# A transformer layer on one core: where the second norm's modulation row is computed, and how the first pieces are loaded

## The chip, the cores and the metric

The kernel runs on one core of one Trainium2 chip. The metric is the device time of one execution in microseconds; the median of three runs stands in the section on the profile. The names of the engines are those of the profile: PE (matmul), PEld (its weight load), DVE (VectorE), ACT (ScalarE), POOL (GpSimd) and SP, which here only issues transfers.

## The reference

One layer over 256 latent tokens and 256 context tokens of width 2048. A conditioning vector gives six modulation chunks of 2048 values by one matrix product each; the branches read a normed and modulated input.

```python
def adaln(cond, w_ada, b_ada):
    return jnp.split(jax.nn.silu(cond) @ w_ada + b_ada, 6, axis=-1)

m_lat, m_ctx = adaln(c, w_ada, b_ada), adaln(c_ctx, w_ada, b_ada)
hc = modulate(rms_norm(ctx, norm1_g), m_ctx[0], m_ctx[1])     # h * (1 + scale) + shift
h  = modulate(rms_norm(x, norm1_g), m_lat[0], m_lat[1])
# pc = hc @ w_in[:, :3072], p = h @ w_in -> keys and values of both, queries and gates of h
o_a = gqa(...)         # 16 heads of 128, 4 key heads, rotary
o_b = diff_attn(...)   # 8 heads; each head's output goes through rms_norm(o, subln_g)
merged = sigmoid(g_a) * (o_a @ w_br_a) + sigmoid(g_b) * (o_b @ w_br_b)
x = x + m_lat[2] * (merged @ w_out)
h = modulate(rms_norm(x, norm2_g), m_lat[3], m_lat[4])        # shift is chunk 3
x = x + m_lat[5] * ((silu(h @ w_ff_gate) * (h @ w_ff_up)) @ w_ff_down)
```

## The kernel before

Every large product goes over weight tiles of 128 x 1024 fp32 (two k-tiles of 128 rows by 512 columns, 512 KB). A tile is loaded by SP into the ring `wraw` (7 buffers), ACT casts it to a high part `whi` (L235), DVE subtracts to get the low part `wlo` (L237), and PE makes three matmuls of 512 columns for each product (L241, L242, L243): high by high, high by low, low by high. The stages follow each other on PE: first the keys and values of latent and context tokens, for which x is modulated on the way (to about 145 us); queries, gates, and the attention of branch B, then of branch A (to about 806 us); the merge, `o_a @ w_br_a` times its gate; the output projection (four groups of 512 columns, 8 weight tiles each, from about 894 to 982 us); then the feed-forward. A scheduler places the instructions of each engine in the order of the code with priorities. Each engine, and SP's queue of transfers, works in order.

**The first modulation chunks (`ada_cond`, L280 to L340).** Chunks 0 and 1 are computed in six steps of `STEPS = ((0, 1), (1, 1), (2, 2), (4, 4), (8, 4), (12, 4))`, (first k-tile, how many), each step just before its columns are needed. A step takes two parts (shift and scale), and for each part the conditioning vectors `cst` times pieces of the matrix, 16 matmuls `ada` (L314). A piece is 512 KB in a host-arranged tensor `ada_t`. The steps of 4 k-tiles have 8 pieces to a part, 2 matmuls to each. In all three of these steps, pieces 0 and 1 share a tile of the pool `big`, pieces 2 and 3 go in halves of 256 KB into four small tiles `wada1` of the scratch tags `nr` (2 buffers) and `p` (4 buffers), and pieces 4 to 7 into `wraw`. All 16 matmuls are issued together after the last piece. Tag `p` also holds the tables `cs` and `used` that POOL reads when it makes the rope tables (`rp_kb` and others).

**The later chunks (`ada_pieces`, `ada_row`).** Chunks 2, 4 and 3, and during the feed-forward chunk 5, are made in 32 pieces of 512 KB each. A piece is loaded into `wraw` (L453), and DVE multiplies it by one value of the vector and adds it to a tile `ada` (`SCALAR_TENSOR_TENSOR`, L459) behind the latest wlo. After the last piece PE sums over the partitions (`adac`), DVE adds the bias, and POOL writes the row to DRAM and broadcasts it (`ada_everywhere`). The generator `later` holds chunks 2, 4, 3; `take(later, 1)` advances it by one step, of which a piece has one. `side_work` calls it on each turn of the attention that has nothing else to do: every second turn before branch A's attention is done in its data (`a_done`), and two of three after; the merge calls it too, but nothing is left by then. `b_all`, the broadcast shift of the second norm, is read by `norm2` at the end of the output projection.

**The output of branch B (L826 to L846).** For each of 16 units PE makes `o`, ACT copies it to `on` and sums its squares (`sso`), DVE scales and shifts the sum to `rstdo` (L123), POOL raises it to the power -1/2 (L124), ACT multiplies `on` by it (L842), and PE transposes `on`.

Of the kernel before, what the change touches and what calls it, by code (L numbers as in the profile page):

```python
# [41 lines left out]
TURN2 = 5  # L42
# [4 lines left out]
def hybrid_block(ctx: ExitStack, tc: tile.TileContext, t: dict, out: bass.AP):  # L47
    nc = tc.nc

    big = ctx.enter_context(tc.tile_pool(name="big", bufs=BIG))  # L50
    wp = ctx.enter_context(tc.tile_pool(name="wp", bufs=3))
# [6 lines left out]
    def big_tile(name, dt=F32):  # L58
        return big.tile([P, 2048], dt, tag="big", name=name)
# [7 lines left out]
    def s_ps(name="s"):  # L67
        return psum.tile([P, CG], F32, tag="s", bufs=2, name=name)

    def scratch(name, n=CG, dt=F32, tag="scr", bufs=3):  # L70
        return scr.tile([P, n], dt, tag=tag, bufs=bufs, name=name)
# [137 lines left out]
        nc.vector.tensor_scalar(out=neglam, in0=neglam, scalar1=-LAM_INIT, scalar2=None, op0=ALU.add)  # L209


    last_hi, last_lo = [], []

    def load_raw(r0, c0, n=2):
        raw = wp.tile([P, WK, CG], F32, tag="wraw", bufs=WRAW, name="wraw")
# [5 lines left out]

    def load_w(src, r0, c0, nk=WK, in_big=False):
        raw = wp.tile([P, WK, CG], F32, tag="wraw", bufs=WRAW, name="wraw")
        nc.sync.dma_start(out=raw[:, 0:nk], in_=src[r0:r0 + nk * P, c0:c0 + CG].rearrange("(k p) c -> p k c", p=P))
        return split_w(raw, nk, in_big)

    def split_w(raw, nk, in_big=False, late=None):
# [52 lines left out]
    def ada_cond(k0, nk):  # L280
        ncol = nk * P
        kk = 2 * CG // ncol
        n0 = k0 * P * 2 * D // (P * 2 * CG)
        mod = []
        for part in range(2):
            aps = s_ps("ada")
            held = []
            for q in range(0, NKT, kk):
                piece = t["ada_t"][n0].rearrange("p (k c) -> p k c", c=ncol)
                n0 += 1  # L290
                n = q // kk
                if nk < 4 or n > 3:
                    wt = wp.tile([P, 2 * CG], F32, tag="wraw", bufs=WRAW, name="wada").rearrange("p (k c) -> p k c", c=ncol)
                    nc.sync.dma_start(out=wt, in_=piece)
                elif n < 2:
                    if n == 0:
                        two = big_tile("wada2").rearrange("p (n k c) -> p n k c", n=2, c=ncol)
                    wt = two[:, n]
                    nc.sync.dma_start(out=wt, in_=piece)
                else:  # L300
                    wt = [scratch("wada1", tag=tag, bufs=b) for tag, b in (("nr", 2), ("p", 4))]
                    for j in range(2):
                        nc.sync.dma_start(out=wt[j], in_=piece[:, j, :])
                held += [(q + j, wt[j] if nk == 4 and 1 < n < 4 else wt[:, j, :]) for j in range(kk)]
                last = q + kk == NKT
                if k0 and not last:
                    if nk == 4 and n == 3:
                        yield None
                    continue
                for k, rhs in held[::-1] if k0 else held:  # L310
                    g = k % 4
                    early, late_k = k < 4, k >= NKT - 4
                    with tc.issue_after(last_pe[0].ins) if k0 == 1 and k == held[-1][0] else nullcontext():
                        last_pe[0] = nc.tensor.matmul(aps[32 * g:32 * g + 32, 0:ncol], lhsT=cst[:, k, :], rhs=rhs,  # L314
                                                      start=late_k if k0 else early, stop=early if k0 else late_k)
                held = []
                if last:
                    asb = scratch("asb")
                    last_asb.append(nc.scalar.copy(out=asb[:, 0:ncol], in_=aps[:, 0:ncol]))
                yield None  # L320
                if last:
                    atp = tp_ps("atp")
                    for j in range(nk):
                        nc.tensor.transpose(out=atp[:, j * P:(j + 1) * P], in_=asb[:, j * P:(j + 1) * P], identity=ident)
                    m = small(f"mod{part}", 8)
                    mv = m[:, 0:2 * nk].rearrange("p (j w) -> p j w", w=2)
                    nc.vector.tensor_reduce(
                        out=mv, in_=atp[:, 0:ncol].rearrange("p (j g m) -> p j m g", g=4, m=32)[:, :, 0:2, :],
                        axis=AX.X, op=ALU.add)
# [213 lines left out]
    a_done = []  # L543
# [258 lines left out]
    def back(br, u, pr):  # L802

        grp, hh = unit(br, u)
        if br == "a":
            if hh % 2 == 0:
                pair[:] = [big_tile("pT", F32R).rearrange("p (k c) -> p k c", k=4) for _ in range(2)]
            pT = list(pair)
        else:
            pT = scratch("pT", tag="pTb", bufs=2).rearrange("p (k c) -> p k c", k=4)  # L810
        for i, p in enumerate(pr):
            tp = tp_ps("ptp")
            for kt in range(4):
                nc.tensor.transpose(out=tp[:, kt * P:(kt + 1) * P], in_=p[:, kt * P:(kt + 1) * P], identity=ident)  # L814
            src = tp.rearrange("p (k q) -> p k q", k=4)
            if br == "a":
                c0 = hh % 2 * SEQ + i * P
                split(*[x[:, :, c0:c0 + P] for x in pT], src)
            else:
                nc.scalar.copy(out=pT, in_=src)  # L820
        yield None
        if br == "a" and hh % 2 == 0:
            return
        op = tp_ps("o")
        if br == "a":
            for kt in range(4):  # L826
                vh, vl = [v[:, kt, grp * AD:(grp + 1) * AD] for v in v_a]
                mm3(op, vh, vl, pT[0][:, kt, :], pT[1][:, kt, :], kt == 0, kt == 3)
            last_o.append(nc.scalar.copy(out=o_raw(grp * 4 + hh - 1, 2), in_=op))
            return  # L830
        vb = acc["vb"][grp].rearrange("p (t c) -> p t c", c=CG)
        tk = u % 2
        on = scratch("on", BV, tag="on", bufs=2)
        for kt in range(4):
            nc.tensor.matmul(op[:, 0:BV], lhsT=pT[:, kt, :], rhs=vb[:, kt, hh * BV:(hh + 1) * BV], start=(kt == 0), stop=(kt == 3))  # L835
        nc.scalar.copy(out=on, in_=op[:, 0:BV])
        junk = scratch("junk_o", tag="sq", bufs=2)
        ss = small("sso", 1)
        nc.scalar.activation(out=junk[:, 0:BV], in_=on, func=AF.Square, accum_out=ss)
        r = rstd_of(ss, 1, BV, "rstdo")  # L840
        yield None
        nc.scalar.mul(out=on, in_=on, mul=r)  # L842
        yield None
        tp = tp_ps("otp")
        nc.tensor.transpose(out=tp[:, 0:P], in_=on, identity=ident)
        nc.scalar.mul(out=o_raw(AH + grp * 4 + hh)[:, tk * P:(tk + 1) * P], in_=tp[:, 0:P], mul=gsub)  # L846
# [15 lines left out]
    turns = [0]  # L862
# [3 lines left out]
    def side_work():  # L866

        if next(chores[-1], chores[-1]) is chores[-1] and not quiet:
            turns[0] += 1
            take(later, 1 if turns[0] % (3 if a_done else 2) else 0)  # L870

    q_order = [("b", g) for g in range(2)] + [("a", g) for g in range(4)]
    others = [(gate_d[w], xT, 0, w_in, (GA0, GB0)[w], cg) for w in range(2) for cg in range(4)]
# [35 lines left out]
    for n, (br, u) in enumerate(units):  # L909
        q = (br, unit(br, u)[0])  # L910
# [31 lines left out]
    w_bra, w_out = t["w_br_a"][0], t["w_out"][0]  # L942
    mT = Parts("mT", NKT)
    for cg in range(4):
# [35 lines left out]
        for k, _ in enumerate(project(w_bra, oT, AH, cg * CG, gated)):  # L980
# [5 lines left out]
                    assert not work  # L986
                    o_parts(3)
            take(gates, 1 if cg else (0, 0, 0, 0, 2, 2, 3, 0)[k])
    drain(later)
    b_all = ada_everywhere("b_all", 2)  # L990


    xn = [big_tile(f"xn{i}") for i in range(2)]
# [78 lines left out]
            take(norm2_of[1], 2)  # L1072

    for cg in range(4):
        drain(project(w_out, mT, NKT, cg * CG, out_evac(cg), **(dict(tail=TURN2, hook=tail_hook, in_big=(6, 7)) if cg == 3 else {})))


    NFT = DFF // P
# [103 lines left out]
```

## Time and profile before

| what | value |
|---|---|
| three runs | 1702.79, 1704.09 (median), 1705.93 us |
| profiled execution | 1703.83 us, of which the span is 1701.7 us |
| granted clock of PE over the span | 0.997 |
| PE / PEld busy | 99% / 80% |
| DVE / ACT / POOL busy | 67% / 46% / 12% |
| mean rate of the transfers | 243 GB/s |
| DVE, wlo and ada | 498 of 1.22 us, 120 of 1.28 us on average |

The profile is of one execution. Its page names each group of instructions as `line engine operation out<-in`, with buffer numbers left out. In a timeline the number in brackets is the time for which the engine stood idle before the instruction, with what ended it. A clock below 1.00 means that PE's matmuls were spaced further apart.

### The profile page before, as it was taken

The numbers are of one execution on the slowest core, as the hardware profiler recorded it, in microseconds if no ns is written. First come the engines' busy times: TensorE is split into PE (matmuls) and PEld (weight loads), VectorE is DVE, ScalarE is ACT, GpSimd is POOL, SyncE is SP. The second block draws the span as 40 slices with busy tenths as digits, with TensorE's granted clock in tenths as the row PEclk, the third lists the DMA queues.
The fourth block names the chain that finished last, engine by engine and source line by source line (L and its number), as shares of the span: only waits on it lengthen the run. The fifth ranks groups of instructions, "written<-read, shape, count | busy, mean of one in ns | idle before, by whom it ended". The sixth has DMA issues, their size and how long they took to land.

```text
span 1701.7 us, 21519 instructions
## 1 busy us (share of the span) xinstructions
PE 1676.8 (99%) x7889; PEld 1355.1 (80%) x7889; DVE 1138.4 (67%) x1438; ACT 779.0 (46%) x1071; POOL 209.3 (12%) x296
## 2 busy tenths in 40 slices
PE   7999999999999999999999999999999999999998
PEld 5677778887887778888888888888888888888887
DVE  5665779798687878996666755566666666554454
ACT  5221222246666656577544534444444444333332
POOL 0200002011231210011111101111111111100000
PEclk9999999999999999999999999999999999999999
DMA  9787875778766768776777857788888888766662
GB/s 352 288 316 275 304 253 157 234 252 256 246 180 216 222 225 272 246 238 212 256 265 237 294 175 221 235 263 267 263 272 263 269 274 253 238 218 195 216 207 88
DMA packets 181860, 413.08 MB, mean 243 GB/s; under 512 B 15065, under 2 KB 16298, under 8 KB 181498
## 3 DMA queue, kind: packets, MB, share of 16 engines
q1 hardware_dynamic: 169482, 374.17, 67.3%
q0 software_dynamic: 12272, 37.53, 7.4%
q8 instruction: 62, 1.02, 0.3%
q14 instruction: 44, 0.36, 0.1%
HBM read 395.35 MB, written 16.29 MB: 242 GB/s over the span
## 4 chain that ended last, share of the span: by engine, by line
PE 75%; issue 10%; DVE 6%; DMA 4%; POOL 3%; ACT 2%; SPq 0%; POOLq 0%; DVEq 0%; ACTq 0%
PE mm L241 22%; PE mm L242 22%; PE mm L243 22%; DVE wlo L237 2%; PE ada L314 1%; POOL fturn L1091 1%; ACT whi L235 1%; PE ptp L814 1%; DMA turn_d<-fpart 1%; DMA fturn<-turn_d 1%; DMA wraw<-in_w_in_dram 1%; DVE ada L459 1%; PE mm L401 1%; PE o L835 1%; DVE mx L736 1%
## 5 line engine op out<-in xcount | busy, mean ns | idle before, releaser
L237 DVE TENSOR_TENSOR wlo<-wraw,whi 128x1024 fp32r<-128x1024 f32 x498 | 606.8, 1220 | 443.9 <-ACT whi L235 442.9
L235 ACT CAST whi<-wraw 128x1024 fp32r<-128x1024 f32 x498 | 522.4, 1050 | 714.0 <-PE mm L243 607.2
L242 PE MATMUL mm<-wlo,hT 128*128 128x512 f32 x684 | 266.3, 389 | 0.1
L243 PE MATMUL mm<-whi,hT 128*128 128x512 f32 x684 | 266.1, 389 | 0.0
L241 PE MATMUL mm<-whi,hT 128*128 128x512 f32 x684 | 266.1, 389 | 0.0
L241 PE MATMUL mm<-whi,xT 128*128 128x512 f32 x630 | 252.7, 402 | 1.3 <-ACT xT L359 1.2
L242 PE MATMUL mm<-wlo,xT 128*128 128x512 f32 x630 | 247.0, 392 | 4.3 <-DVE wlo L237 4.3
L243 PE MATMUL mm<-whi,xT 128*128 128x512 f32 x630 | 246.9, 392 | 0.0
L459 DVE SCALAR_TENSOR_TENSOR ada<-wada,vt,ada 128x1024 f32<-128x1024 f32 x120 | 152.0, 1277 | 0.0
L242 PEld LDWEIGHTS mm<-wlo,hT 128*128 128x128 f32 x684 | 128.4, 188 | 27.7 <-DVE wlo L237 0.9
L241 PEld LDWEIGHTS mm<-whi,hT 128*128 128x128 f32 x684 | 128.4, 188 | 26.7
L243 PEld LDWEIGHTS mm<-whi,hT 128*128 128x128 f32 x684 | 128.4, 188 | 26.5
L241 PEld LDWEIGHTS mm<-whi,xT 128*128 128x128 f32 x630 | 118.6, 188 | 32.7 <-issue 7.0
L242 PEld LDWEIGHTS mm<-wlo,xT 128*128 128x128 f32 x630 | 118.8, 189 | 28.2 <-DVE wlo L237 5.7
L243 PEld LDWEIGHTS mm<-whi,xT 128*128 128x128 f32 x630 | 118.5, 188 | 26.0 <-DVE xT L360 0.3
L241 PE MATMUL mm<-whi,fT 128*128 128x512 f32 x354 | 137.5, 388 | 0.5 <-DVE y L1127 0.5
L242 PE MATMUL mm<-wlo,fT 128*128 128x512 f32 x354 | 137.3, 388 | 0.0
L243 PE MATMUL mm<-whi,fT 128*128 128x512 f32 x354 | 137.3, 388 | 0.0
L241 PEld LDWEIGHTS mm<-whi,fT 128*128 128x128 f32 x354 | 66.4, 188 | 15.0 <-issue 0.8
L243 PEld LDWEIGHTS mm<-whi,fT 128*128 128x128 f32 x354 | 66.5, 188 | 13.8
L242 PEld LDWEIGHTS mm<-wlo,fT 128*128 128x128 f32 x354 | 66.4, 188 | 13.7
L241 PE MATMUL mm<-whi,oT 128*128 128x512 f32 x192 | 75.9, 396 | 0.0
(236 smaller groups left out, 2150.4 us busy)
## 6 DMA issues: line engine op xcount, KB each, us to landing
wraw<-in_w_in_dram SPq DMA_DIRECT2D x159, 512.0 KB, 4.7
wada<-in_w_ada_dram SPq DMA_DIRECT2D x128, 512.0 KB, 4.6
wraw<-in_w_ff_gate_dram SPq DMA_DIRECT2D x88, 512.0 KB, 4.6
wraw<-in_w_ff_up_dram SPq DMA_DIRECT2D x88, 512.0 KB, 5.4
wraw<-in_w_ff_down_dram SPq DMA_DIRECT2D x88, 512.0 KB, 4.8
wada<-in_ada_t_dram SPq DMA_DIRECT2D x52, 512.0 KB, 7.8
wraw<-in_w_br_a_dram SPq DMA_DIRECT2D x32, 512.0 KB, 5.3
wraw<-in_w_out_dram SPq DMA_DIRECT2D x32, 512.0 KB, 5.2
```

Of the source, the lines that this page charges most:

```text
L235: last_hi.append(nc.scalar.copy(out=hi[:, 0:nk], in_=raw[:, 0:nk]))
L237: last_lo.append(nc.vector.tensor_tensor(out=lo[:, 0:nk], in0=raw[:, 0:nk], in1=hi[:, 0:nk].bitcast(F32), op=ALU.subtract))
L241: nc.tensor.matmul(ps, lhsT=ah, rhs=wh, start=first, stop=False, skip_group_check=skip)
L242: nc.tensor.matmul(ps, lhsT=ah, rhs=wl, start=False, stop=False, skip_group_check=skip)
L243: return nc.tensor.matmul(ps, lhsT=al, rhs=wh, start=False, stop=last, skip_group_check=skip)
L314: last_pe[0] = nc.tensor.matmul(aps[32 * g:32 * g + 32, 0:ncol], lhsT=cst[:, k, :], rhs=rhs, start=late_k if k0 else early, stop=early if ...
L401: last_pe[0] = nc.tensor.matmul(ps[cg], lhsT=x, rhs=ws0[cg][y], start=(n == 0), stop=(n == 2))
L459: nc.vector.scalar_tensor_tensor(out=dst, in0=wt, scalar=sc[:, 0, kt:kt + 1], in1=dst, op0=ALU.mult, op1=ALU.add)
L736: nc.vector.tensor_reduce(out=mx, in_=sp, axis=AX.X, op=ALU.max, negate=True)
L814: nc.tensor.transpose(out=tp[:, kt * P:(kt + 1) * P], in_=p[:, kt * P:(kt + 1) * P], identity=ident)
L835: nc.tensor.matmul(op[:, 0:BV], lhsT=pT[:, kt, :], rhs=vb[:, kt, hh * BV:(hh + 1) * BV], start=(kt == 0), stop=(kt == 3))
L1091: nc.gpsimd.dma_start(out=whole[32 * b:32 * b + 32].rearrange("p (k a j) -> p k a j", k=4, a=4), in_=blocks[b])
```

## The change

Four edits, with this effect on the order of the instructions:
- The step of the k-tiles 4 to 7 takes all 8 pieces of a part through `wraw`, and its matmuls come in two batches of 8, after pieces 3 and 7 (`first_ks` and `last_ks` set where the accumulation starts and stops). In the two last steps the halves of pieces 2 and 3 go into `nr` twice, `sq` and `pTb` instead of `nr`, `nr`, `p`, `p`, and their loads are put behind the last weight tile's load.
- The multiplication by `rstdo` is done on DVE, as `TENSOR_SCALAR`, instead of on ACT.
- In the attention, every third turn takes a step of `later`.
- In the output projection, each of the steps of the first two groups takes a step of `later`; what is left of it and the broadcast `b_all` come ahead of the third group.

```diff
-    last_hi, last_lo = [], []
+    last_hi, last_lo, last_load = [], [], []
...
-        nc.sync.dma_start(out=raw[:, 0:nk], in_=src[...])
+        last_load.append(nc.sync.dma_start(out=raw[:, 0:nk], in_=src[...]))
...
-                if nk < 4 or n > 3:
-                    wt = wp.tile([P, 2 * CG], F32, tag="wraw", ...)
-                    nc.sync.dma_start(out=wt, in_=piece)
...
-                    wt = [scratch("wada1", tag=tag, bufs=b) for tag, b in (("nr", 2), ("p", 4))]
+                with tc.issue_after(last_load[-1].ins) if k0 >= 8 else nullcontext():
+                    if k0 < 8 or n > 3:
+                        wt = wp.tile([P, 2 * CG], F32, tag="wraw", ...)
+                        nc.sync.dma_start(out=wt, in_=piece)
...
+                        wt = [scratch("wada1", tag=tag, bufs=2) for tag in (("nr", "nr") if n == 2 else ("sq", "pTb"))]
...
-                if k0 and not last:
-                    if nk == 4 and n == 3:
+                if k0 and not last and (k0 != 4 or n != 3):
+                    if k0 >= 8 and n == 3:
                         yield None
                     continue
+                first_ks, last_ks = (range(0, 4), range(12, 16)) if k0 == 0 else (range(4, 8), range(8, 12)) if k0 == 4 else (range(12, 16), range(0, 4))
...
-                                                      start=late_k if k0 else early, stop=early if k0 else late_k)
+                                                      start=k in first_ks, stop=k in last_ks)
...
-        nc.scalar.mul(out=on, in_=on, mul=r)
+        nc.vector.tensor_scalar(out=on, in0=on, scalar1=r, scalar2=None, op0=ALU.mult)
...
-            take(later, 1 if turns[0] % (3 if a_done else 2) else 0)
+            take(later, 1 if turns[0] % 3 == 0 else 0)
...
-    drain(later)
-    b_all = ada_everywhere("b_all", 2)
...
     for cg in range(4):
-        drain(project(w_out, mT, NKT, cg * CG, out_evac(cg), ...))
+        if cg == 2:
+            drain(later)
+            b_all = ada_everywhere("b_all", 2)
+        for _ in project(w_out, mT, NKT, cg * CG, out_evac(cg), ...):
+            take(later, 1)
```

SP's queue in the first 60 us, at the step of the k-tiles 4 to 7. `wraw` is a weight tile, `wada` a piece in the ring, and `wada_737` to `wada_860` are halves of pieces in small tiles. Before:

```order
L224 DMA wraw<-in_w_in_dram 128x2x512
L303 DMA wada_737<-in_ada_t_dram 128x512
L303 DMA wada_738<-in_ada_t_dram 128x512
L303 DMA wada_741<-in_ada_t_dram 128x512
L303 DMA wada_742<-in_ada_t_dram 128x512
L224 DMA wraw<-in_w_in_dram 128x2x512
L294 DMA wada<-in_ada_t_dram 128x1024
L303 DMA wada_860<-in_ada_t_dram 128x512
L294 DMA wada<-in_ada_t_dram 128x1024 x3
```

And now (lines of the changed file are shifted by one):

```order
L224 DMA wraw<-in_w_in_dram 128x2x512
L295 DMA wada<-in_ada_t_dram 128x1024 x4
L224 DMA wraw<-in_w_in_dram 128x2x512
L295 DMA wada<-in_ada_t_dram 128x1024
L170 DMA tok_t_686<-in_x_t_dram 128x1024
L170 DMA tok_t_686<-in_ctx_t_dram 128x1024
L295 DMA wada<-in_ada_t_dram 128x1024 x3
L224 DMA wraw<-in_w_in_dram 128x2x512
L295 DMA wada<-in_ada_t_dram 128x1024 x4
```

The halves are gone from this step, and four whole pieces stand ahead of its weight tile.

DVE in branch B's attention, at the run of work ahead of the matmul at 574.93 us. `mm` is a finished projection whose norm and rotary position (`ss`, `nr`, `sq`) are made here. Before:

```order
L237 TENSOR_TENSOR wlo<-wraw,whi 128x1024
L123 TENSOR_SCALAR rstdo<-sso 128x1
L459 SCALAR_TENSOR_TENSOR ada_2770<-wada_5070,vt,ada_2770 128x1024
L492 TENSOR_REDUCE ss<-sq 128x4
L501 TENSOR_TENSOR nr<-mm,rp_qa 128x512
```

And now:

```order
L460 SCALAR_TENSOR_TENSOR ada_2800<-wada_4966,vt,ada_2800 128x1024
L237 TENSOR_TENSOR wlo<-wraw,whi 128x1024
L123 TENSOR_SCALAR rstdo<-sso 128x1
L843 TENSOR_SCALAR on<-on,rstdo 128x128
L493 TENSOR_REDUCE ss<-sq 128x4
L502 TENSOR_TENSOR nr<-mm,rp_qa 128x512
```

The piece has moved to before the wlo, and the multiplication stands between `rstdo` and the rest of the run.

DVE at the seam of the merge and the output projection, where `m` and `gin` are the merge's products, `mT` the transposed result. Before:

```order
L237 TENSOR_TENSOR wlo<-wraw,whi 128x1024 x4
L966 TENSOR_TENSOR gin<-mm,gin 128x512 x2
L967 TENSOR_TENSOR m_7823<-m_7823,gin 128x512
L967 TENSOR_TENSOR m_7893<-m_7893,gin 128x512
L237 TENSOR_TENSOR wlo<-wraw,whi 128x1024 x2
L247 TENSOR_TENSOR mT_8012<-mtp,mT_8012 128x4x128
```

And now:

```order
L460 SCALAR_TENSOR_TENSOR ada_6631<-wada_7924,vt,ada_6631 128x1024
L237 TENSOR_TENSOR wlo<-wraw,whi 128x1024
L967 TENSOR_TENSOR gin<-mm,gin 128x512 x2
L968 TENSOR_TENSOR m_7759<-m_7759,gin 128x512
L968 TENSOR_TENSOR m_7829<-m_7829,gin 128x512
L460 SCALAR_TENSOR_TENSOR ada_6631<-wada_7962,vt,ada_6631 128x1024
L237 TENSOR_TENSOR wlo<-wraw,whi 128x1024
L247 TENSOR_TENSOR mT_7958<-mtp,mT_7958 128x4x128
L460 SCALAR_TENSOR_TENSOR ada_6631<-wada_7990,vt,ada_6631 128x1024
```

An ada now stands by each wlo, where before there was none. 28 pieces have moved to these two stages, 16 to the merge and 12 to the projection.

More of the change, by code (lines that the diff above doesn't have):

```diff
@@ L223, in load_w @@
         raw = wp.tile([P, WK, CG], F32, tag="wraw", bufs=WRAW, name="wraw")
-        nc.sync.dma_start(out=raw[:, 0:nk], in_=src[r0:r0 + nk * P, c0:c0 + CG].rearrange("(k p) c -> p k c", p=P))
+        last_load.append(nc.sync.dma_start(out=raw[:, 0:nk], in_=src[r0:r0 + nk * P, c0:c0 + CG].rearrange("(k p) c -> p k c", p=P)))
         return split_w(raw, nk, in_big)
@@ L291, in ada_cond @@
                 n = q // kk
-                if nk < 4 or n > 3:
[L293 to L300, printed above, removed]
-                    wt = [scratch("wada1", tag=tag, bufs=b) for tag, b in (("nr", 2), ("p", 4))]
-                    for j in range(2):
-                        nc.sync.dma_start(out=wt[j], in_=piece[:, j, :])
@@ L304, in ada_cond @@
-                held += [(q + j, wt[j] if nk == 4 and 1 < n < 4 else wt[:, j, :]) for j in range(kk)]
+                with tc.issue_after(last_load[-1].ins) if k0 >= 8 else nullcontext():
+                    if k0 < 8 or n > 3:
+                        wt = wp.tile([P, 2 * CG], F32, tag="wraw", bufs=WRAW, name="wada").rearrange("p (k c) -> p k c", c=ncol)
+                        nc.sync.dma_start(out=wt, in_=piece)
+                    elif n < 2:
+                        if n == 0:
+                            two = big_tile("wada2").rearrange("p (n k c) -> p n k c", n=2, c=ncol)
+                        wt = two[:, n]
+                        nc.sync.dma_start(out=wt, in_=piece)
+                    else:
+                        wt = [scratch("wada1", tag=tag, bufs=2) for tag in (("nr", "nr") if n == 2 else ("sq", "pTb"))]
+                        for j in range(2):
+                            nc.sync.dma_start(out=wt[j], in_=piece[:, j, :])
@@ L305, in ada_cond @@
+                held += [(q + j, wt[j] if k0 >= 8 and 1 < n < 4 else wt[:, j, :]) for j in range(kk)]
                 last = q + kk == NKT
-                if k0 and not last:
-                    if nk == 4 and n == 3:
+                if k0 and not last and (k0 != 4 or n != 3):
+                    if k0 >= 8 and n == 3:
                         yield None
                     continue
+                first_ks, last_ks = (range(0, 4), range(12, 16)) if k0 == 0 else (range(4, 8), range(8, 12)) if k0 == 4 else (range(12, 16), range(0, 4))
@@ L310, in ada_cond @@
                 for k, rhs in held[::-1] if k0 else held:
                     g = k % 4
-                    early, late_k = k < 4, k >= NKT - 4
                     with tc.issue_after(last_pe[0].ins) if k0 == 1 and k == held[-1][0] else nullcontext():
                         last_pe[0] = nc.tensor.matmul(aps[32 * g:32 * g + 32, 0:ncol], lhsT=cst[:, k, :], rhs=rhs,
-                                                      start=late_k if k0 else early, stop=early if k0 else late_k)
+                                                      start=k in first_ks, stop=k in last_ks)
@@ L1074, in hybrid_block @@
     for cg in range(4):
-        drain(project(w_out, mT, NKT, cg * CG, out_evac(cg), **(dict(tail=TURN2, hook=tail_hook, in_big=(6, 7)) if cg == 3 else {})))
+        if cg == 2:
+            drain(later)
+            b_all = ada_everywhere("b_all", 2)
+        for _ in project(w_out, mT, NKT, cg * CG, out_evac(cg), **(dict(tail=TURN2, hook=tail_hook, in_big=(6, 7)) if cg == 3 else {})):
+            take(later, 1)
     NFT = DFF // P
```

## Prediction

> **What bounds the kernel now.** I read the page first, then PE's idle time in stretches of 20 us, and then the timeline around each stretch with a gap.
>
> ```profile
> PE 1676.8 (99%) x7889; PEld 1355.1 (80%) x7889; DVE 1138.4 (67%) x1438; ACT 779.0 (46%) x1071; POOL 209.3 (12%) x296
> ...
> PE 75%; issue 10%; DVE 6%; DMA 4%; POOL 3%; ACT 2%; SPq 0%; POOLq 0%; DVEq 0%; ACTq 0%
> ```
>
> PE is busy for 99% of a span of 1701.7 us, and the change removes no matmul. So the time can change only where PE stands still or runs at a lower clock. The stretches that show either, apart from the first and the last 20 us (columns: length, busy time of PE, PEld, DVE, ACT, POOL, granted clock, DMA share, GB/s):
>
> ```profile
> 60.00:80.00 20.00, 16.13 (x71) 11.38 (x73) 11.71 (x23) 3.02 (x6) 1.78 (x9) 0.91 0.86 325
> ...
> 500.00:520.00 20.00, 19.28 (x98) 15.07 (x98) 18.51 (x36) 15.19 (x29) 2.94 (x4) 1.00 0.57 164
> ...
> 560.00:580.00 20.00, 17.02 (x82) 12.85 (x81) 17.88 (x34) 12.59 (x29) 6.69 (x4) 0.91 0.56 174
> ...
> 620.00:640.00 20.00, 18.71 (x87) 15.19 (x87) 18.27 (x31) 12.27 (x21) 2.03 (x2) 1.00 0.53 161
> ```
>
> PE is idle for 3.87, 0.72, 2.98 and 1.29 us in them, and in two of them the granted clock is 0.91. The change touches the first, and it reorders VectorE's work in the three others.
>
> **Part 1: tiles and load order of the first pieces (60 to 80 us).** SP's queue, then its longest wait there (us in all, times, longest):
>
> ```profile
> 51.19 0.33 SPq L294 DMA_DIRECT2D wada<-in_ada_t_dram  x1
> 61.81 0.33 SPq L303 DMA_DIRECT2D wada<-in_ada_t_dram  x1
> ...
> 63.68 0.57 SPq L224 DMA_DIRECT2D wraw<-in_w_in_dram  x1
> ```
>
> ```profile
> SPq L303 <- POOL rp_kb L198: 10.1, 1, 10.1
> ```
>
> Half a piece, loaded at L303 into a small tile that POOL's rope tables still use, blocks SP from 51.5 to 61.8 us. Queued behind it are three pieces and a weight tile, whose issue slips to 63.68. The DMA engines stand still meanwhile:
>
> ```profile
> 56.00:60.00 4.00, 4.00 (x44) 2.57 (x43) 4.00 (x8) 1.42 (x2) 4.00 (x10) 1.00 0.13 50
> ...
> 64.00:80.00 16.00, 13.35 (x60) 9.43 (x62) 7.71 (x13) 1.71 (x3) 0.00 (x0) 0.89 1.01 392
> ```
>
> At 50 GB/s the transfers cannot be what is short; it is the issue. The weight tile's way on, by ACT, DVE and PE:
>
> ```profile
> 70.83 1.04 ACT L235 CAST whi<-wraw 128x1024 fp32r<-128x1024 f32 x1 [5.84 <-DMA wraw<-in_w_in_dram]
> ```
>
> ```profile
> 71.90 1.23 DVE L237 TENSOR_TENSOR wlo<-wraw,whi 128x1024 fp32r<-128x1024 f32 x1 [5.20 <-ACT whi L235]
> 73.05 2.48 DVE L442 TENSOR_TENSOR kb<-mm,kb 128x512 f32<-128x512 f32 x4
> ```
>
> ```profile
> 62.66 0.50 PE L241 MATMUL mm<-whi,xT 128*128 128x512 f32 x1 [1.22 <-ACT xT L359]
> ...
> 73.79 0.50 PE L241 MATMUL mm<-whi,cT 128*128 128x512 f32 x1 [2.65 <-DVE kb L442]
> ...
> 77.46 0.47 PE L241 MATMUL mm<-whi,cT 128*128 128x512 f32 x1
> 77.77 0.40 PE L242 MATMUL mm<-wlo,cT 128*128 128x512 f32 x1
> 78.00 0.39 PE L243 MATMUL mm<-whi,cT 128*128 128x512 f32 x1
> 78.32 3.64 PE L314 MATMUL ada<-wada,cst 128*32 128x512 f32 x32
> ```
>
> PE needs the PSUM bank that the kb addition empties, the addition stands behind wlo on DVE, and wlo waits for the late weight tile. That is 2.65 us. From 73.79 to 78.32 the 12 matmuls of a weight tile then take 4.53 us; part 3 shows 2.72 us for such a tile, so another 1.81 us go to the halved pace after the gap. With the 1.22 us at 62.66 that is 5.68 us.
>
> By the Trainium skill ("TensorE: Matmul & The Clock Gate", Part 1) the clock is halved only after an idle window of about 3.4 us, so that a gap of 2.65 us need not do it. If by that rule the slow matmuls have another cause, they stay (rival E). This trace shows the slow pace straight behind the gap and a granted clock of 0.91 there, so I count it to the gap.
>
> The changed order puts the pieces of this chunk into ring buffers, and no small tile waits for POOL. SP's next waits are for a ring buffer: the third and fourth piece wait for the last ada matmul of the piece before (near 57 us), and the weight tile of 50.56 us comes behind them at about 57.9 us. Following each buffer to its last reader I find every tile just in time, and the late weight tile about 6 us earlier. The pieces now feed PE in batches of 4 and 8 instead of 16. By the row at 78.32 the 32 records of 16 steps take 3.64 us, so the first batch of 4 takes 0.91 us; it stands just before the matmul at 62.66, where 1.22 us were idle. The bounds: 5.68 us if all is regained, and 3.5 us if the batch waits about 0.9 us for its pieces and a later tile another 1.3 us. A loss is possible only by rival A. I take 5.3 us, nearer the upper end, because SP has those 10.1 us more in which to issue.
>
> **Part 2: VectorE scales, and fewer pieces, in the attention.** DVE around the gap at 575 us, ACT's multiplication there, its wait over all 16, and PE:
>
> ```profile
> 564.89 1.23 DVE L237 TENSOR_TENSOR wlo<-wraw,whi 128x1024 fp32r<-128x1024 f32 x1 [0.44 <-ACT whi L235]
> 566.03 0.15 DVE L123 TENSOR_SCALAR rstdo<-sso 128x1 f32<-128x1 f32 x1
> 566.09 1.28 DVE L459 SCALAR_TENSOR_TENSOR ada<-wada,vt,ada 128x1024 f32<-128x1024 f32 x1
> 567.28 0.68 DVE L492 TENSOR_REDUCE ss<-sq 128x4 f32<-128x512 f32 x1
> 567.88 0.68 DVE L501 TENSOR_TENSOR nr<-mm,rp_qa 128x512 f32<-128x512 f32 x1
> ...
> 573.67 1.21 DVE L237 TENSOR_TENSOR wlo<-wraw,whi 128x1024 fp32r<-128x1024 f32 x1
> 574.80 0.74 DVE L797 SCALAR_TENSOR_TENSOR p<-p,rs 128x512 f32<-128x512 f32 x1
> ```
>
> ```profile
> 567.81 0.40 ACT L842 ACTIVATE on<-on,rstdo 128x128 f32<-128x128 f32 x1 [1.87 <-POOL rstdo L124]
> ```
>
> ```profile
> ACT on L842 <- POOL rstdo L124: 33.0, 16, 4.0
> ```
>
> ```profile
> 568.06 0.39 PE L242 MATMUL mm<-wlo,xT 128*128 128x512 f32 x1
> ...
> 574.93 0.50 PE L242 MATMUL mm<-wlo,xT 128*128 128x512 f32 x1 [2.98 <-DVE wlo L237]
> ```
>
> ```profile
> 636.58 0.50 PE L242 MATMUL mm<-wlo,xT 128*128 128x512 f32 x1 [1.29 <-DVE wlo L237]
> ```
>
> ```profile
> 395.00:616.00 221.00, 217.30 (x1087) 172.66 (x1086) 172.51 (x266) 137.73 (x266) 49.96 (x43) 0.99 0.71 224
> ```
>
> The multiplication itself is cheap on DVE: between 0.15 us (128x1) and 0.68 us (128x512, both above); I take 0.25 for 128x128, nearer the small end, 4 us for 16. The wait is not cheap. DVE works in order, and in 11 of the 16 places the multiplication now stands directly behind the rstdo that POOL has to turn into a power. ACT waited 33.0/16 = 2.06 us for that; from the end of rstdo at 566.18 to 567.81 it was 1.63 us. So DVE stands still for 18 to 23 us, with the next wlo queued behind it. Against that, one in three turns takes a piece where one in two did: 24 ada operations between the first and last rstdo become 14, at 1.19 us each (566.09 to 567.28) 12 us less. DVE goes from 172.5 us busy to about 185 us taken of 221.
>
> Where it matters: the gap at 575 us comes from the run of work on DVE ahead of the wlo at 573.67. In the changed order an ada leaves that run and a multiplication with its wait enters, +0.25 + 1.6 - 1.19, about +0.7 us. For the gap at 636.58 an ada leaves, and no multiplication enters: 1.29 us regained. ACT no longer waits, which brings some whi earlier. From below, both gaps go, with the 1.8 us of slow clock: -6. From above, +6 (rival C). I take -0.5.
>
> **Part 3: pieces in the merge and the output projection.** 28 pieces move here, 16 into the merge (4 to each group of 8 weight tiles) and 12 behind the first 12 tiles of the projection. Before:
>
> ```profile
> 894.00:916.00 22.00, 22.00 (x99) 18.22 (x98) 13.22 (x14) 10.02 (x13) 3.27 (x6) 1.00 0.65 208
> 916.00:938.00 22.00, 22.00 (x99) 18.22 (x98) 13.22 (x14) 10.02 (x13) 3.27 (x6) 1.00 0.82 275
> ```
>
> ```profile
> 899.95 1.22 DVE L237 TENSOR_TENSOR wlo<-wraw,whi 128x1024 fp32r<-128x1024 f32 x1 [1.50 <-ACT whi L235]
> 902.67 1.23 DVE L237 TENSOR_TENSOR wlo<-wraw,whi 128x1024 fp32r<-128x1024 f32 x1 [1.50 <-ACT whi L235]
> ```
>
> ```profile
> 904.33 0.39 PE L242 MATMUL mm<-wlo,mT 128*128 128x512 f32 x1
> ```
>
> ```profile
> wraw<-in_w_out_dram SPq DMA_DIRECT2D x32, 512.0 KB, 5.2
> ```
>
> A tile comes every 2.72 us, and wlo, ready at 901.17, is first read at 904.33: 3.16 us of lead. Nothing is idle on PE, so at best this part is free.
> - DVE: wlo and ada take 1.13 (573.67 to 574.80) + 1.19 = 2.32 of 2.72 us. In the dense run at the seam, 15 wlo, 15 ada and 12 operations of 0.60 us (567.28 to 567.88) need 42.0 us in 15 x 2.72 = 40.8 us. By the order of the queue it is late by 2 to 2.7 us at the worst place, under the lead of 3.16.
> - DMA: a piece is as large as a weight tile, 0.524 MB in 2.72 us = 193 GB/s. The first group needs 208 + 193 = 401 GB/s, the second 275 + 193 = 468, against the 392 that the queue reached above. That puts the transfers behind by 0.06 us for 8 tiles and 0.53 us for 4, 2.6 us. The ring of 7 buffers goes round in 9.5 us at two a tile; less 5.2 us of landing and 2.3 us of cast and subtraction it leaves 2.0 us, and with the lead 5.2 us of cover.
> - The broadcast of the finished row moves from before the merge to the third group. It is read in the second norm, near 966 us, some 40 us later.
>
> From below 0; from above 2.6 + 2.7 = 5.3 us if both show in full. I take +1.0.
>
> **The sum.** 1703.83 - 5.3 - 0.5 + 1.0 = 1699.0 us. 1703.83 us is the profiled execution (its span of 1701.7 and 2.1 outside it), 0.26 under the median of the runs.
>
> **The rivals.**
> - A. The first gap only moves, so that the change's first part doesn't do what it says: sixteen pieces and the weights share one ring of 7, and the tile of 50.56 us is issued 7 us later. If that tile makes PE wait, 0 to 2 us are gained in place of 5.3: 1702 to 1704. For it: the load is 392 GB/s once it runs. Against it: the 10.1 us in which SP issued nothing.
> - B. The output projection loses its lead, as the DVE backlog and the transfers add up: +3 to +5.3 instead of +1.0, 1701 to 1703.5. It decides when a piece lands more than 5 us later than the 5.2 us of now.
> - C. The wait for POOL makes wlo late, which ends on the slower side. In the second half of this phase leads are short (the wlo that ended at 566.12 was read at 568.06, 1.9 us later), and 5 of the 11 waits of 2.06 us fall there. At about 1.4 us of PE each, and 1.8 us for one more slow clock, it is +9: 1708. It decides once a wlo with less than 2 us of lead stands behind such a wait. Against it: ACT is freed of the same wait, and 10 ada are gone.
> - D. The gap at 575 us closes because whi and the ada work before it come out earlier: -3 to -5, 1694 to 1696.
> - E. The slow matmuls behind 73.79 us stay when the gap goes: 1.81 us less, 1700.8. Against it: the slow pace (4.53 us for 12 matmuls) ends at 77.46, a few microseconds after PE went on (77.46 to 77.77 is 0.31, and 77.77 to 78.00 is 0.23).
>
> The Trainium skill ("DMA: Bandwidth & Descriptors", Specifications) limits a core's HBM traffic to about 358 GB/s; by that figure the projection would fall behind by 0.33 x 8 + 0.84 x 4 = 6.0 us, just over its cover, and B would be the likeliest. The 392 GB/s over 16 us above is more than the page allows, so I leave B at its chance.
>
> **How the numbers follow.** The forecast, 1696 to 1700.6 us: 0.56. A 0.12, B 0.14, C 0.10, D 0.05, E 0.03. A change of 0.2%, 3.4 us, is about what a measurement of this kernel can tell from none. Faster: the forecast and D, 0.61. Same: A, E, B but for 0.02, and 0.02 of C, 0.29. Slower: the rest of B and C, 0.10. The range of 1693 to 1706 us takes in D, A and B and leaves out most of C.
>
> **What would show it.** Right: SP's wait of 10.1 us is gone, the row at 73.79 has no idle time, and 60 to 80 us shows a clock of 1.00; DVE has a wait for POOL of 18 to 23 us; PE's gap at 575 us is there, that at 636 is not; and 894 to 938 us shows PE without a gap at over 390 GB/s. Wrong: a PE wait for an ada piece or weight tile before 100 us (A), for wlo after 890 us (B), or several for wlo between 500 and 620 us (C).

## The result and the profile after

The changed kernel takes 1695.39 us (median of 6 runs, 1694.65 to 1698.16), against 1703.44 us for the kernel before in 6 runs (1700.08 to 1705.93). The ratio is 0.9956, with a 95% interval of 0.9943 to 0.9969: 8.0 us less. The profiled execution took 1694.65 us, with a span of 1692.9. From its page:

```profile
span 1692.9 us, 21508 instructions
...
PE 1673.2 (99%) x7889; PEld 1352.7 (80%) x7889; DVE 1144.9 (68%) x1454; ACT 776.2 (46%) x1055; POOL 195.7 (12%) x296
```

PE has as many instructions as before, and 3.6 us less busy time, most of it the slow matmuls behind the gaps at 73.79 and 574.93 us (1.8 and 1.5 us). The stretches that the prediction started from, now (same columns):

```profile
60.00:80.00 20.00, 19.40 (x99) 12.74 (x98) 13.22 (x23) 4.41 (x7) 0.00 (x0) 1.00 0.86 326
560.00:580.00 20.00, 18.81 (x98) 14.96 (x97) 17.92 (x32) 11.78 (x25) 2.56 (x3) 1.00 0.52 161
500.00:520.00 20.00, 20.00 (x106) 15.87 (x105) 18.75 (x35) 14.72 (x29) 2.61 (x3) 1.00 0.58 173
620.00:640.00 20.00, 20.00 (x98) 16.65 (x97) 15.79 (x21) 10.47 (x16) 1.01 (x1) 1.00 0.67 203
```

The clock is 1.00 in all of them. To see where the time went, I took the matmul that first reads the wlo of the same weight tile in both traces, and subtracted its times:

| weight tile | before, us | after minus before, us | what lies between |
|---|---|---|---|
| 4 | 45.2 | -0.9 | the first pieces land sooner, mostly by chance (below) |
| 12 | 103.3 | -4.6 | part 1: SP's wait |
| 30 | 214.8 | -5.4 | a short wait only the trace of before has |
| 105 | 504.8 | -5.3 | |
| 170 | 755.1 | -11.9 | part 2: attention of B |
| 200 | 859.0 | -13.2 | 1.2 of this is moved work (the sum of the third row), repaid below |
| 214 | 898.9 | -11.4 | part 3: seam of merge and projection |
| 230 | 942.4 | -7.8 | part 3: first two groups of the projection |
| 500 | 1683.3 | -8.6 | |

So the time came from the start (-3.7 us) and above all from the attention (-6.7 us), and the merge and projection gave back about 4.1 us (11.9 less 7.8).

**Start.** SP's queue and the stretch in which the transfers stood still:

```profile
56.16 0.80 SPq L295 DMA_DIRECT2D wada<-in_ada_t_dram  x2
57.05 0.39 SPq L224 DMA_DIRECT2D wraw<-in_w_in_dram  x1
57.53 0.42 SPq L295 DMA_DIRECT2D wada<-in_ada_t_dram  x1
```

```profile
56.00:60.00 4.00, 4.00 (x41) 2.77 (x34) 3.09 (x10) 0.37 (x1) 3.75 (x13) 1.00 0.71 230
```

```profile
61.17 1.06 PE L315 MATMUL ada<-wada,cst 128*32 128x512 f32 x8 [0.60 <-DMA wada<-in_ada_t_dram]
62.16 0.50 PE L241 MATMUL mm<-whi,xT 128*128 128x512 f32 x1
```

SP's wait of 10.1 us for POOL is gone. SP now waits for ring buffers, up to 7.9 us, until 56.16, as the prediction said, but the weight tile goes out at 57.05 us instead of 63.68. Transfers run at 230 GB/s where they ran at 50, the first batch of ada stands in the old gap of 1.22 us, of which 0.60 us are left, and there is no gap near 73 us.

**Attention.** The tile `rstdo` on POOL, before (first row) and after (second; min/median/max in ns), DVE's wait for it, and DVE at one of the places where an ada stands between:

```profile
L124 POOL TENSOR_TENSOR rstdo<-rstdo,neghalf x16: 548/1456/3204, 395.4 to 614.6; 128x1 f32<-128x1 f32 x16
```

```profile
L124 POOL TENSOR_TENSOR rstdo<-rstdo,neghalf x16: 548/558/1528, 390.5 to 601.7; 128x1 f32<-128x1 f32 x16
```

```profile
DVE on L843 <- POOL rstdo L124: 9.2, 15, 0.7
```

```profile
567.57 0.15 DVE L123 TENSOR_SCALAR rstdo<-sso 128x1 f32<-128x1 f32 x1
567.63 1.28 DVE L460 SCALAR_TENSOR_TENSOR ada<-wada,vt,ada 128x1024 f32<-128x1024 f32 x1
569.36 0.29 DVE L843 TENSOR_SCALAR on<-on,rstdo 128x128 f32<-128x128 f32 x1 [0.45 <-POOL rstdo L124]
```

The operation on POOL is the same, and its median fell from 1.46 to 0.56 us. DVE waits 9.2 us, at most 0.7 at a time, where 18 to 23 us were forecast. PE's gaps in this stretch are gone but for one:

```profile
577.56 1.16 PE L836 MATMUL o<-vb,pT 128*128 128x128 f32 x8 [1.19 <-DVE qT L247]
```

**Merge and projection.** Two stretches, the longest wait of ACT in 860 to 925 us, its wait for the merge's tiles from 806 to 890 us, and PE:

```profile
860.00:900.00 40.00, 38.67 (x176) 31.79 (x175) 35.84 (x36) 15.71 (x18) 2.97 (x6) 1.00 1.01 368
900.00:925.00 25.00, 23.49 (x104) 17.55 (x103) 19.91 (x23) 11.49 (x16) 5.80 (x11) 1.00 1.01 352
```

```profile
ACT whi L235 <- DMA wraw<-in_w_out_dram: 26.6, 14, 3.9
```

```profile
ACT whi L235 <- DMA wraw<-in_w_br_a_dram: 15.8, 9, 2.4
```

```profile
875.43 0.63 PE L975 MATMUL mtp<-ident,m 128*128 128x128 f32 x4 [1.33 <-DVE m L968]
...
901.96 0.50 PE L242 MATMUL mm<-wlo,mT 128*128 128x512 f32 x1 [0.72 <-DVE wlo L237]
905.50 0.50 PE L242 MATMUL mm<-wlo,mT 128*128 128x512 f32 x1 [0.50 <-DVE wlo L237]
915.46 0.50 PE L242 MATMUL mm<-wlo,mT 128*128 128x512 f32 x1 [0.29 <-DVE wlo L237]
```

The DMA engines are busy all the time (share 1.01) and move 352 to 368 GB/s on average. Tiles come late already in the merge: ACT waits nine times for one of `w_br_a`, where in the kernel before it never does between 806 and 890 us. The four waits make 2.84 us of idle time on PE. By the starts of the matmuls around them the same four places lose 3.8 of the 4.1 us, since a restart costs a little more than the idle time that is shown.

### The profile page after: what moved, and what is told of

It is laid out like the page before. It is cut to its first block, busy times and chain, and to the rows that moved or that the text cites. A ratio compares the mean times of both kernels' runs of the same rounds, so it can differ in the third digit from the quotient of the medians.

```text
span 1692.9 us, 21508 instructions
## 1 busy us (share of the span) xinstructions
PE 1673.2 (99%) x7889; PEld 1352.7 (80%) x7889; DVE 1144.9 (68%) x1454; ACT 776.2 (46%) x1055; POOL 195.7 (12%) x296
## 3 DMA queue, kind: packets, MB, share of 16 engines
q8 instruction: 62, 1.02, 0.2%
## 4 chain that ended last, share of the span: by engine, by line
PE 91%; DMA 3%; DVE 3%; issue 1%; ACT 1%; POOL 0%; SPq 0%; ACTq 0%; DVEq 0%; POOLq 0%
PE mm L241 27%; PE mm L242 27%; PE mm L243 27%; DMA wraw<-in_w_out_dram 2%; PE ada L315 2%; PE ptp L815 1%; DVE wlo L237 1%; PE o L836 1%; PE mm L402 1%; ACT whi L235 1%; DMA wada<-in_ada_t_dram 1%; PE s L791 1%; PE s L241 0%; PE o L241 0%; PE s L243 0%
```

## The experiments

The theory after the result: SP's wait cost what was forecast; the scaling on DVE gained several microseconds, since ACT is freed and POOL answers sooner than forecast; the moved pieces gain a little in the attention and lose more to the transfers behind it. The rivals stand with each run.

**Parts alone.** These four ran beside the kernel before (1702.54 us, 23 runs). First the tags alone:

```diff
-  wt = [scratch("wada1", tag=tag, bufs=b) for tag, b in (("nr", 2), ("p", 4))]
+  wt = [scratch("wada1", tag=tag, bufs=2) for tag in (("nr", "nr") if n == 2 else ("sq", "pTb"))] if k0 == 4 else [... as before]
```

> The kernel before, with one edit: at the step of the k-tiles 4 to 7, pieces 2 and 3 use the scratch tags nr, nr, sq and pTb instead of nr, nr, p, p. Order, batches and the ring stay as before. Theory (the wait of SP for POOL's tables is what costs at 60 to 80 us): SP's wait of 10.1 us at L303 goes, PE's gap of 2.65 us and the slow matmuls behind it go, the gap of 1.22 us stays; 4.5 us less, about 1699. Rival (the ring and the batches do it, the wait is hidden): no change, 1703. Second rival (the gap only moves to the next late tile): 0 to 2 us less.

Measured: 1697.48 us, ratio 0.9972 (0.9960 to 0.9984), 5.1 us less. In the list of SP's waits the one for POOL is gone, no gap is left near 73 us, and the one at 62 us stays:

```profile
62.34 0.50 PE L241 MATMUL mm<-whi,xT 128*128 128x512 f32 x1 [1.08 <-ACT xT L359]
```

Taking away the shared tag alone gives the whole gain of part 1. Ring and batches aren't needed for it.

The whole of part 1, with the scaling and the pieces as before:

> The kernel before with part 1 alone: the changed tiles, batches and load order of the first pieces; the scaling stays on ACT and the later pieces stay in the attention. Theory: the part's gain as seen in the trace of the changed kernel, 4.85 us at 60 to 80 us, and the gaps at 516.9, 574.9 and 636.6 us stay (0.6, 3.0, 1.3 us); 1698 to 1699. Rival (some of the 5 us gained in the attention comes from the start having been shifted against the attention): the gaps in the attention shrink here too, 1694 to 1696.

Measured: 1699.57 us, ratio 0.9986 (0.9976 to 0.9996), 3.0 us less, a little under what was expected. The gaps in the attention stay (0.62, 2.79, 1.85 us, and another of 0.71 at 582), so the gain there is not a shifted start. At 62 us the ring is no better than the tags: PE waits for a piece, for 1.24 us here and 0.60 in the changed kernel, and the batch follows this wait instead of filling it, where x_tags waits 1.08 us for xT. The five batches also take 7.9 us (twice 1.06 and three times 1.92) where two of 3.64 us did the same work.

```profile
62.41 1.06 PE L315 MATMUL ada<-wada,cst 128*32 128x512 f32 x8 [1.24 <-DMA wada<-in_ada_t_dram]
```

The scaling alone:

```diff
-        nc.scalar.mul(out=on, in_=on, mul=r)
+        nc.vector.tensor_scalar(out=on, in0=on, scalar1=r, scalar2=None, op0=ALU.mult)
```

> The kernel before with part 2a alone: the multiplication by rstdo on DVE, nothing else. Theory (DVE's wait is short, because POOL's power takes 0.56 us while DVE stands still against 1.46 us while DVE works): of 16 powers at least 10 take under 0.6 us, DVE waits for POOL 7 to 11 us in all, ACT is freed, and the gaps at 575 and 637 us shrink but stay above 0.5 us: 0 to 3 us less. Rival (the wait of 18 to 23 us that was forecast, which was hidden only by there being fewer pieces): DVE waits over 15 us, gaps for wlo grow by 2 us or more, slower by 2 to 5 us.

Measured: 1697.30 us, ratio 0.9971 (0.9959 to 0.9982), 5.2 us less, more than expected. DVE's wait for POOL, and the matmul that waited 2.98 us in the kernel before:

```profile
DVE on L842 <- POOL rstdo L124: 7.0, 13, 0.7
```

```profile
568.22 0.50 PE L242 MATMUL mm<-wlo,xT 128*128 128x512 f32 x1
```

The part of the theory about the power failed: here its median is 1.47 us, since at 10 of the 16 places an ada or a wlo of DVE runs beside it. The wait is short all the same, since that operation stands between rstdo and the multiplication and covers it. A gap of 0.55 us comes one tile later, at 573.29, and the one at 630 us stays, at 1.84 us.

Why the gap closed can be followed in the two traces. Before, ACT's multiplication waits for POOL, the cast of the next tile stands behind it in ACT's queue, and DVE waits for that cast:

```profile
556.37 0.40 ACT L842 ACTIVATE on<-on,rstdo 128x128 f32<-128x128 f32 x1 [2.36 <-POOL rstdo L124]
556.67 1.03 ACT L235 CAST whi<-wraw 128x1024 fp32r<-128x1024 f32 x1
```

```profile
557.74 1.22 DVE L237 TENSOR_TENSOR wlo<-wraw,whi 128x1024 fp32r<-128x1024 f32 x1 [1.82 <-ACT whi L235]
```

With the scaling on DVE the same cast starts at 549.11 and the same wlo at 550.38 us:

```profile
550.38 1.22 DVE L237 TENSOR_TENSOR wlo<-wraw,whi 128x1024 fp32r<-128x1024 f32 x1
```

That is 7.4 us earlier, where PE is only 3.95 us earlier. The run of work ahead of the gap then starts 6.9 us earlier (559.12 against 566.03), so 3 us earlier than before as PE sees it, and that is the size of the gap.

Not all of the gain is due to the edit. In the profiled executions, 2.9 us of the difference lie before 215 us, where nothing was changed (the gap at 73 us was 2.21 us and no slow matmuls followed), and 4.0 us between tiles 105 and 170. How far chance goes there, x_tags shows: it changes nothing in the attention and differs by 1.5 us.

The pieces alone:

```diff
-            take(later, 1 if turns[0] % (3 if a_done else 2) else 0)
+            take(later, 1 if turns[0] % 3 == 0 else 0)
...
+        for _ in project(w_out, mT, NKT, cg * CG, out_evac(cg), ...):
+            take(later, 1)
```

> The kernel before with the move of the pieces alone: one in three turns in the attention, 16 pieces in the merge and 12 in the output projection. Theory (the gain of 5.2 us in the attention comes from the ada operations that left VectorE; the loss of 2.8 us in merge and projection comes from the transfers that came): gaps in the attention total 1.5 us or less against 4.9 before plus 1.8 of slow matmuls, gaps from 870 to 920 us total 2 to 4 us; 1699 to 1702. Rival (the gain comes from ACT being freed by the scaling): the gaps at 575 and 637 us stay as before and the loss remains, 1705 to 1707.

Measured: 1703.63 us, ratio 1.0008 (0.9999 to 1.0018): 1.1 us more, at the edge of what can be told from nothing. Neither theory had it whole. The gap that stood at 637 us is gone, where x_scale has 1.84 us: so it is the pieces that close it. Gaps at 513, 569 and 583 us stay (0.61, 1.06, 2.52 us), and the loss in the projection is there:

```profile
582.95 2.06 PE L835 MATMUL o<-vb,pT 128*128 128x128 f32 x8 [2.52 <-DVE qT L247]
...
908.95 0.50 PE L242 MATMUL mm<-wlo,mT 128*128 128x512 f32 x1 [1.07 <-DVE wlo L237]
912.49 0.50 PE L242 MATMUL mm<-wlo,mT 128*128 128x512 f32 x1 [0.51 <-DVE wlo L237]
```

-3.0, -5.2 and +1.1 add up to -7.1 us, against -8.0 for all parts together; each has some 2 us of uncertainty.

**Transfers or VectorE in the merge and projection.** The next four ran together (before: 1703.20 us, 7 runs). First fewer bytes:

```diff
+            n = 256 if chunk == 3 else 1024
-            nc.sync.dma_start(out=wt, in_=w_ada[..., 1024 columns])
+            nc.sync.dma_start(out=wt[:, 0:n], in_=w_ada[..., n columns])
...
+            if chunk == 3:   # DVE still on 1024 columns
+                wt = wt[:, 0:256].unsqueeze(1).to_broadcast([P, 4, 256])
```

> The changed kernel, with the 32 pieces of chunk 3 (28 of them in merge and projection) loading 256 of their 1024 columns; DVE still works on 1024 columns, reading the 256 four times, so the second norm's shift is not the reference's. Theory (transfers take the lead in the merge and the output projection, 4.2 us): the gaps at 875 to 916 us go but for under 0.5 us, the rate from 860 to 900 us falls under 320 GB/s; 1690.5 to 1692. Rival (VectorE's backlog does it): the gaps stay within 0.5 us of 2.8, 1695.

Measured: 1692.82 us, ratio 0.9940 (0.9925 to 0.9955). No gap over 0.15 us is left from 860 to 925 us, and the transfers have room from 860 to 900:

```profile
860.00:900.00 40.00, 40.00 (x182) 33.11 (x181) 38.47 (x39) 17.51 (x22) 4.37 (x8) 1.00 0.83 260
```

Then less work on DVE:

```diff
+            if chunk == 3 and kt > 0:
+                wt, dst = wt[:, 0:256], dst[:, 0:256]
```

> The changed kernel, with DVE working on only 256 of the 1024 columns of each piece of chunk 3 from its second k-tile on; the transfers stay whole, and three quarters of the shift are left unfinished. Theory (transfers): the tiles are as late, the gaps at the three places that wait for wlo stay above 1.5 us together, the one at 875 us that waits for DVE's m shrinks; 1693.5 to 1695. Rival (VectorE): all gaps go, 1690.5 to 1692.

Measured: 1694.96 us, ratio 0.9949 (0.9932 to 0.9965). DVE has much time to spare, the transfers none, and PE still waits:

```profile
860.00:900.00 40.00, 39.98 (x179) 32.33 (x179) 27.03 (x37) 15.47 (x18) 2.73 (x6) 1.00 1.00 367
```

```profile
907.88 0.50 PE L242 MATMUL mm<-wlo,mT 128*128 128x512 f32 x1 [0.67 <-DVE wlo L237]
```

By the times of the same matmuls, this kernel still loses 2.7 us from 860 to 942 us, y_dma 0.6 and the changed kernel 4.1, without the 1.2 us of moved work. So the transfers are the larger cause. The gap at 875 us behind the merge's products is gone here, and in y_dma too: it takes both, late tiles and DVE's added work. At the three other places the waits make 1.1 us together, less than expected.

The same 28 pieces, spread evenly:

```diff
-            if k > 3:                    # merge: 4 of 8 tiles
+            if k % 8 not in (0, 3, 6):   # 5 of 8
                 take(later, 1)
...
-            take(later, 1)
+            take(later, k % 2 if cg < 2 else 1)
```

> The changed kernel, with the same 28 pieces spread evenly: 20 in the merge (5 of each 8 tiles) and 8 in the projection, one to every second tile of the first two groups. By the rows of before that is 265 + 121 = 386 GB/s in the merge, 305 and 372 in the two groups. Theory (the peak of the demand, over 392 GB/s, is what costs): the gaps from 860 to 920 us go to under 0.5 us, 1690.5 to 1692. Rival (any extra transfers here cost, whatever their order): 2 us or more of gaps remain, 1694 to 1696.

Measured: 1693.23 us, ratio 0.9941 (0.9927 to 0.9956). There is no gap in these stretches; one of 0.46 us for wlo stands at 951 us:

```profile
810.00:860.00 50.00, 50.00 (x230) 41.42 (x229) 44.94 (x47) 24.95 (x31) 7.67 (x14) 1.00 1.02 368
860.00:900.00 40.00, 40.00 (x183) 33.11 (x182) 33.18 (x36) 18.28 (x23) 4.37 (x8) 1.00 0.98 340
900.00:925.00 25.00, 25.00 (x113) 19.52 (x112) 20.21 (x22) 10.83 (x13) 4.44 (x8) 1.00 1.00 356
```

So here it was the order of the pieces, not their number, that cost. From 806 to 942 us this kernel loses 0.3 us where the changed kernel loses 4.2, again without the moved work. The time lies above the 1690.5 to 1692 that was expected, and its interval overlaps with that of the changed kernel; the trace is what shows the gaps gone.

The two edits that gained most, without the move of the pieces:

> The kernel before with the two edits that gained most alone: the four scratch tags of the step of the k-tiles 4 to 7, and the scaling on DVE; the pieces stay where they were. Theory (the two add up, as they act at different places: 5.1 and 5.2 us): 1692 to 1694, so below the changed kernel; gap at 637 us remains (1.6 to 1.9 us). Rival (both measured the same share of chance, the slow clock behind gaps): 1695 to 1697.

Measured: 1692.74 us, ratio 0.9940 (0.9925 to 0.9954), 10.5 us less: 5.1 and 5.2 add up. The gap of 1.33 us at 626 us remains.

**All good forms together**, with the changed kernel beside it (before: 1703.65 us, 11 runs):

> The changed kernel with two of its parts taken in the form that did better: pieces spread evenly as in y_spread, and the step of the k-tiles 4 to 7 as before but for the four scratch tags (x_tags). Theory (the pieces in the ring cost up to 1 us of waiting at 62 us, where the tags cost none; the parts add up): 0.3 to 1.5 us below y_spread, 1691.5 to 1693, and 2.5 to 4 us below the changed kernel run beside it. Rival (what is left is chance from run to run): within 0.7 us of y_spread.

> The changed kernel itself, word for word, run again beside z_best, so that the two are compared on one chip: 1694.5 to 1696.

Measured: 1693.35 us, ratio 0.9944 (0.9931 to 0.9956), and 1696.69 us, ratio 0.9960 (0.9948 to 0.9973), for the changed kernel. The rival held: z_best is no better than y_spread or y_tags_scale. The three can't be told apart; by the medians of their ratios all lie 2 to 3 us below the changed kernel, though the intervals overlap. In whole times it made no difference whether the pieces were moved. The traces show two effects that cancel: between tiles 105 and 170 z_best and y_spread gain 6.7 us and y_tags_scale, without the move, 5.0, and from 806 to 942 us z_best loses 1.7 us, although its pieces are spread as in y_spread. Part of that is a wait for DVE in the merge:

```profile
851.75 0.63 PE L974 MATMUL mtp<-ident,m 128*128 128x128 f32 x4 [0.81 <-DVE m L967]
```

Why it stands in one of the two kernels only is open.

**POOL and the second input of DVE.** In the traces the powers of 0.56 us stood where DVE was idle or ran a sum over one tensor. To test it:

```diff
         r = rstd_of(ss, 1, BV, "rstdo")
+        if u % 2 == 0:
+            nc.vector.tensor_tensor(out=dum[:, 0:512], in0=vb[:, 0, :], in1=vb[:, 1, :], op=ALU.mult)
+        else:
+            nc.vector.tensor_reduce(out=dum, in_=vb[:, 0, :], axis=AX.X, op=ALU.add)
```

> The changed kernel with one more DVE operation of 128x512 directly behind each rstdo, its result thrown away: for even units a product of two tensors, for odd units a sum over one tensor, both of 0.68 us. Theory (POOL's power waits while DVE reads two tensors, not while it reads one): POOL's rstdo takes 0.9 to 1.2 us in 8 places and 0.56 us in 8. Rival (any DVE work slows POOL alike): all 16 alike, 0.9 us or more. Second rival (DVE's work has no effect, and the long powers had another cause): 0.56 us in most, with no relation to the operation.

Measured, in one execution of 1693.95 us: POOL took 0.87 to 0.94 us in the 8 places with two tensors and 0.55 to 0.56 us in the 8 with one. One of each, with DVE beside it:

```profile
390.62 0.94 POOL L124 TENSOR_TENSOR rstdo<-rstdo,neghalf 128x1 f32<-128x1 f32 x1 [20.96 <-DVE rstdo L123]
...
401.22 0.56 POOL L124 TENSOR_TENSOR rstdo<-rstdo,neghalf 128x1 f32<-128x1 f32 x1 [7.99 <-DVE rstdo L123]
```

```profile
390.46 0.68 DVE L844 TENSOR_TENSOR junk_d<-vb 128x512 f32<-128x512 f32 x1
...
401.06 0.67 DVE L847 TENSOR_REDUCE dumr<-vb 128x1 f32<-128x512 f32 x1
```

The long power ends 0.42 us after DVE's operation (391.56 against 391.14), so POOL seems to be held until DVE is done. The Trainium skill ("GPSIMD Engine Reference", Specifications) says that POOL shares its SBUF interfaces with VectorE and contends with operations that have two SBUF inputs. This run agrees.

## Why the prediction was right or wrong

The forecast was 1699.0 us, faster, in a range of 1693 to 1706; measured were 1695.39 us. The direction and the range held, but two terms of three were mis-sized, and it is luck that their errors partly cancel. The time lies just outside the forecast's own 1696 to 1700.6 us. Of the signs, SP's wait, the matmul at 73.79, the clock and the gap at 636 us came as said; DVE's wait, the gap at 575 us and the projection without a gap did not.

- **Part 1, -5.3 us.** The place, the cause and the chain from SP to PE held; x_tags shows the cause alone, at 5.1 us. In the changed kernel this term measured -3.7 us between the tiles at 45 and 103 us (x_tiles, whole runs: 3.0 us), near the lower bound of 3.5: the first batch waits for its piece (0.60 us here, 0.44 to 1.39 in other runs with this start). Rival A's sign, that wait, was there, but the gap did not simply move: 3.7 us were gained, not 0 to 2. Most of the other 0.9 us at the start is chance: PE's wait for the first piece was 5.75 us before and 4.91 after, and 6.10 in another run of the changed kernel.
- **The slow matmuls** (rival E) went with the gap. But they are no fixed price: behind gaps of 2.65 and 2.98 (before), 2.59 (x_tags) and 2.52 us (x_pieces) some matmuls started 0.43 us apart instead of 0.23, behind 2.79 (x_tiles) and 2.21 us (x_scale, at 73 us) none did. All of these gaps are shorter than the 3.4 us that the prediction cites from the Trainium skill ("TensorE: Matmul & The Clock Gate", Part 1), so the measurement decides against that border here. Nor does the slow pace come in every run: of 41 more runs of the kernel before, the four with a granted clock of 1.000 took 1700.2 to 1700.8 us, the five with 0.996 took 1703.6 to 1705.4.
- **Part 2, -0.5 us, is the step that failed most:** it measured -6.7 us in the trace (1.5 of them the slow matmuls), and for the scaling alone -5.2 in whole runs and -4.0 in the trace. The prediction took DVE's wait from ACT's, 1.63 to 2.06 us a time. ACT's wait was long because at 10 of the 16 places DVE went on with ada or wlo meanwhile. Where DVE itself stands still, POOL needs 0.56 us; where an ada stands between, it covers the wait. So 9.2 us came in place of 18 to 23. The multiplication took 0.29 us (0.25 forecast), and the gap at 637 us went as forecast, by the pieces. The gap at 575 us, which was to grow by 0.7 us, closed, because ACT's cast no longer waits for POOL and the work ahead of the gap starts earlier; in its stretch one of 1.19 us is left. That was rival D, mechanism and time, at 0.05. Rival C rested on the same wait and fell with it.
- **Part 3, +1.0 us,** measured about +4.1, in the range up to 5.3 and at rival B's price. Two steps of it failed. One is the rate: the prediction took 392 GB/s from 64 to 80 us, and the queue reached 368 and 352 here. The other is where the transfers' sum begins. DVE's sum counts the last tiles of the merge, the transfers' sum only the projection; but by the 258 GB/s of 810 to 860 us before, the merge's tiles with a piece ask for 258 + 193 = 451 GB/s, and late tiles come from the merge on. (The projection's first matmul before is at 884.1 us, not at about 894, and its last at 973.7.) B was given 0.14 and was right as a mechanism; its time did not come about, because part 2 gained more. The Trainium skill's figure of 358 GB/s ("DMA: Bandwidth & Descriptors", Specifications), which the prediction set aside for that row, was the better one for this stage: the means of the two stretches bracket it. That the limit it names is the cause isn't shown. It is half a stack's rate, for two cores, this kernel runs on one, and for 10 us the same stage moved more:

```profile
886.00:896.00 10.00, 10.00 (x46) 8.28 (x45) 9.05 (x9) 3.85 (x4) 0.00 (x0) 1.00 1.02 383
```

- **The rest.** The broadcast of the third row cost nothing that the trace shows. The -0.8 us between 188 and 215 us appears in every other run too, so the trace of before was slow there by chance; what it waited for is open.

## What to carry to other kernels

When work moves to another engine, its wait does not move with it unchanged: ask what made the old wait long, here the very engine that was to wait next, and what stood in the queue behind the old wait. A tile in a shared scratch tag ties a transfer to whatever reads the tag; the longest wait of the issuing queue pointed at 5 us that a different tag gave back. And work that fills idle bandwidth should be spread: the same 28 pieces cost 4 us in a bunch and 0.3 or 1.7 us evenly.

## What the runs showed of the hardware

POOL's operation on 128x1 takes 0.55 to 0.57 us beside an idle VectorE or one that sums one tensor, and 0.87 to 3.2 us when one that goes through two is already under way. It then ends about 0.42 us after that operation; at some places it was held through the next ones too (3.20 us at 576.42 us before, behind three in a row). The transfers of these stages, weights mixed with POOL's loads and stores, move 340 to 368 GB/s on average over 25 to 50 us with a DMA share of 0.98 to 1.02. Gaps of 2.5 to 3 us on PE slowed the matmuls behind them, from 0.23 to 0.43 us apart, in 4 of 5 cases.
